# A two-layer mixture-of-experts encoder on one core: router logits with swapped operands, first masks and picks moved, warm-up matmuls at the head, new order of the tail

## Chip, cores and metric

The kernel runs on one core of one Trainium2 chip. The metric is the device time of one execution in microseconds (us), the median of three runs. All times below are us from the first instruction of one profiled execution unless they are marked otherwise.

## What is computed

512 tokens of width 1024 pass through two layers. Each layer has a mixing part (attention with dilated windows, gated MLP, pooling) and a routed expert part; all weights come from HBM. What matters here is the routing and the end of a layer:

```python
def _route(x_flat, router_w, router_bias):
    scores = jax.nn.sigmoid((x_flat @ router_w).astype(jnp.float32))
    biased = (scores + router_bias).reshape(T, N_EXPERT_GROUPS, EXPERTS_PER_GROUP)
    group_score = lax.top_k(biased, TOP_K)[0].sum(-1)
    gsel = jnp.argmax(group_score, axis=-1)
    in_group = biased[jnp.arange(T), gsel]
    _, local = lax.top_k(in_group, TOP_K)
    ...
    gates = sel / sel.sum(-1, keepdims=True)

def reference(x, ...):
    for l in range(DEPTH):                       # 2
        h = _mixing_sublayer(x, ...)
        x = _layernorm(DEEPNORM_ALPHA * x + h, ln1_g[l], ln1_b[l])
        h = _moe(x, router_w, router_bias, w_gate[l], w_up[l], w_down[l])   # 16 experts, top 2, SwiGLU, width 512
        x = _layernorm(DEEPNORM_ALPHA * x + h, ln2_g[l], ln2_b[l])
    return x
```

## The kernel before

Every large product is made of three passes in fp32r (`mm3`): a matrix is split into a rounded part and a remainder, and high times high, high times low and low times high are added in PSUM. ScalarE makes the rounded half of a weight piece (`emit_hi`, L184, tile `whi`), VectorE the remainder (`emit_lo`, L192, tile `wlo`). One half piece (128 x 1024) feeds six matmuls of 512 columns. There are four buffers of each (`NS = 4`), so the split of a half waits until TensorE has used the half four before it. All instructions are written out by hand in one order (a manual schedule): each engine works through its own in the order of the code, and waits where an operand is not there.

The head (L1182 on) loads the first inputs and weights and splits them; TensorE starts as they land.

Between mixing and experts stands the router, for four tiles of 128 tokens. `out2` finishes the output projection, `norm1(i)` normalises tile i and writes it to two places in DRAM. `logits(i)` turns the tile with eight transposes (L257), ScalarE copies them out of PSUM in two halves (L686), sixteen matmul passes in fp32 (eight products of two passes, L689) multiply with `router_w` as the weights loaded into the array (16 columns), and ScalarE takes the exponential of the 16 x 128 result. `scored` turns two such results back with a transpose each (L697) and VectorE adds 1 (L698). `route` ranks the experts on VectorE (some 13 small operations for two tiles), `place` counts positions with small matmuls, `pull(i)` adds tile i's rows of expert 0 into two PSUM banks (`b0`; 16 passes, L779). Then `early` makes the masks of experts 1 and 2 (`mark`, L770), calls `gates` (four operations on VectorE, L760 to L764, then four on GpSimd, L765 and L746 to L749, the last of which write the gate columns of `vg`), and for experts 1 and 2 picks the row numbers (`pick`, L841, four matmuls each, which read column 0 of `vg`) and starts the gathers of their rows from DRAM (L853, issued by GpSimd). `pull(3)` and `turn(0)` (expert 0's rows from PSUM into `gh`, `gl`) follow, then the expert loop.

In the loop, expert 0's `up_piece(0, 0)` and `(0, 1)` (24 matmuls) are followed by `front(1)` and `front(2)`: picks of three columns each, which read all of `vg`.

At the end of a layer the last two experts (14 and 15, `LAST`) are not scattered; `down_piece` writes their products to the two banks `bankY`, `finish_y` scales and splits them (L965 on ScalarE, L966 on VectorE), and `add_last` adds them per tile with matmuls and forms the LayerNorm's statistics, in a way given by `MODE`: "F" and "C" by `bn_stats` on VectorE, "P" by copying and squaring on ScalarE with sums (L1103, L1111) and two small GpSimd operations (L1112, L1113). `norm` scales and shifts. In the last layer `down_piece` of expert 15 runs the four halves for the first 512 columns, then for the second, and each normalised tile goes to `out`.

Of the kernel before, what the change touches and what calls it, by code (L numbers as in the profile page):

```python
# [59 lines left out]
def encoder(ctx, tc, a, out):  # L60
# [9 lines left out]
    LAST = (NE - 2, NE - 1)  # L70
    MODE = ("FPCC", "FFPP")
    cp = pool(ctx, "cp")
# [28 lines left out]
    def load_consts():  # L101
        nc.sync.dma_start(cb, a["consts"])
        nc.sync.dma_start(rw, a["router_w"])
        nc.sync.dma_start(rb, a["router_b"])
        G.memset(one16, 1.0)
        G.memset(mhalf, -0.5)
# [172 lines left out]
    def layer(l, xst, xh, xl, tail):  # L279
# [400 lines left out]

        eTs = {}

        def logits(i):
            xT = tp.tile([128, NK, 128], F32, name="rxT")
            for j in range(2):
                A.activation(xT[:, 4 * j:4 * j + 4, :], transpose4(bankT(), xs[i], j), AF.Copy)  # L686
            b = bankY()
            for k in range(NK):
                T.matmul(b[0:NE, 0:128], rw[:, k, :], xT[:, k, :], start=k == 0, stop=k == NK - 1)  # L689
            eTs[i] = rp.tile([NE, 128], F32, name="eT", bufs=4)  # L690
            A.activation(eTs[i], b[0:NE, 0:128], AF.Exp, scale=-1.0)

        def scored(i0, i1):
            b = bankY()
            bv = b[:, 0:NT * NE].rearrange("p (i e) -> p i e", e=NE)
            for i in range(i0, i1):
                T.transpose(bv[:, i, :], eTs.pop(i), ident[0:NE, 0:NE])  # L697
            V.tensor_scalar(sc[:, i0:i1], bv[:, i0:i1], 1.0, None, op0=OP.add)  # L698

# [20 lines left out]
        def route(i0, i1, E=V):  # L720
            n = i1 - i0
            g4 = lambda t: t[:, i0:i1].rearrange("p i (g e) -> p (i g) e", e=4)
            r = lambda t: t[:, i0:i1]
            E.reciprocal(r(sc), r(sc))
            E.tensor_tensor(r(bi), r(sc), rb[:, None, :].to_broadcast([128, n, NE]), op=OP.add)
            ranks(E, g4(rk), g4(bi), 4 * n)
            E.scalar_tensor_tensor(r(bi), r(rk), 1.5, r(bi), op0=OP.is_lt, op1=OP.mult)
            E.tensor_reduce(r(gs).rearrange("p i g -> p (i g)"), g4(bi), axis=AX.X, op=OP.add)
            ranks(E, r(gr), r(gs), n)
            E.tensor_scalar(r(gr), r(gr), 0.5, None, op0=OP.is_lt)  # L730
            grb = r(gr).rearrange("p i g -> p (i g)")[:, :, None].to_broadcast([128, 4 * n, 4])
            E.scalar_tensor_tensor(g4(m16), g4(rk), 1.5, grb, op0=OP.is_lt, op1=OP.mult)
# [52 lines left out]

        def norm1(i, between=None):
            stats = ln_stats(xs[i], tp)
            if between is not None:
                between()
            ln_apply(xs[i], gb1, stats, True)  # L790
# [145 lines left out]
        def down_piece(e, n):  # L936
            if n == 0:
                ES[e]["y"] = (bankY(), bankY())
            hh, hl = ES[e]["hT"]
            if e == NE - 1 and l + 1 == L:  # L940
                if n == 0:
                    w = [half(("e", l, e, 4 + k // 2), k % 2, NS - k) for k in range(4)]
                    for j in range(2):
                        ws = slice(j * 512, (j + 1) * 512)
                        for k in range(4):
                            mm3(ES[e]["y"][j][0:CAP], hh[:, k], hl[:, k], w[k][0][:, ws], w[k][1][:, ws], k == 0, k == 3)
                return
# [140 lines left out]

        def add_last(i):
            sums = None  # L1090
            if MODE[l][i] == "P":
                sums = sp.tile([128, 4], F32, name="sums", bufs=3)
            for j in range(2):
                js = slice(j * 512, (j + 1) * 512)
                b = bankT()
                if sums is not None:
                    T.matmul(b, ident, xs[i][:, js], start=True, stop=False)
                for e in LAST:
                    lhs = ES[e]["qT"][:, i * 128:(i + 1) * 128]
                    T.matmul(b, lhs, ES[e]["yl"][0][:, js], start=sums is None and e == LAST[0], stop=False)  # L1100
                    T.matmul(b, lhs, ES[e]["yl"][1][:, js], start=False, stop=e == LAST[1])
                if sums is not None:
                    A.activation(xs[i][:, js], b, AF.Copy, accum_out=sums[:, j:j + 1])  # L1103
                else:
                    V.tensor_tensor(xs[i][:, js], xs[i][:, js], b, op=OP.add)
            if sums is None:
# [7 lines left out]
            return None, t  # L1114

        stats = {}

        def prep(i):
# [3 lines left out]
            if MODE[l][i] == "C":  # L1122
                ln_center(xs[i], stats[i])

        def norm(i):
            if MODE[l][i] == "P":
                x, t = xs[i], stats[i][1]
                V.scalar_tensor_tensor(x, x, t[:, 2:3], gb2[0], op0=OP.add, op1=OP.mult)
                V.scalar_tensor_tensor(x, x, t[:, 1:2], gb2[1], op0=OP.mult, op1=OP.add)
            else:  # L1130
                ln_apply(xs[i], gb2, stats[i], MODE[l][i] == "F")

        prep(0)
        if l + 1 == L:
            for i in range(NT):
                prep(i + 1)
                norm(i)
                nc.sync.dma_start(out[i * 128:(i + 1) * 128, :], xs[i])
            ost.close()
            lst.close()  # L1140
            return None
        splits_to(stream["use"] + NS)
        norm(0)
# [162 lines left out]
```

## Time and profile before

| | |
|---|---|
| median of three runs | 1105.14 us (1104.51 to 1105.29) |
| profiled execution, its own time | 1104.96 us |
| span of its instructions | 1103.3 us |
| TensorE matmuls busy | 1055.1 us (96%) |
| VectorE, ScalarE, GpSimd busy | 883.8, 740.2, 413.7 us |
| mean granted TensorE clock | 0.994 |

The time is read from the chain of waits of TensorE: the other engines are free for a good part of the span, so an edit counts where it shortens or lengthens an idle stretch of TensorE, or what runs after its last matmul. A line of a timeline gives start, duration, engine, line, operation, written and read tiles with their shape, a count if equal instructions were merged, and in brackets how long the engine was idle before and whose end it waited for.

### The profile page before, as it was taken

The page shows a single profiled execution, that of the slowest core. Times are in us where ns is not written, and L with a number is a line of the kernel's source. Part 1 is how long each engine was busy: PE and PEld are TensorE (multiplying, and loading weights), DVE is VectorE, ACT ScalarE, POOL GpSimd, SP SyncE. Part 2 cuts the span into 40 slices and gives each one's busy share as a digit, 9 for nine tenths or more (in the row PEclk, how much of TensorE's full clock was granted, in tenths as well). Part 3 has the DMA queues.
Part 4 walks back from the last instruction along what each step waited for, and adds up shares of the span by engine and source line. Part 5 has one row for each costly group of instructions (what it writes and reads, how often), then busy time and mean ns, then how long its engine had stood idle before and what let it go on. Part 6 is the DMA issues. An engine that isn't in the chain of part 4 may idle for free.

```text
span 1103.3 us, 14619 instructions
## 1 busy us (share of the span) xinstructions
PE 1055.1 (96%) x5160; PEld 817.1 (74%) x5160; DVE 883.8 (80%) x1279; ACT 740.2 (67%) x1020; POOL 413.7 (37%) x325
## 2 busy tenths in 40 slices
PE   7999999999999999999899999899899999999995
PEld 5887776777777777777578877777777777777773
DVE  4433898879999999999756249878899999999996
ACT  4334877248888888888542358862578888888872
POOL 0294554232343525230125836433224343334102
PEclk9999999999999999999899999999999999999998
DMA  8162113979999999995313422249799999999831
GB/s 292 65 229 79 68 57 128 399 272 361 351 369 357 373 350 350 361 352 178 114 45 119 150 77 77 77 154 397 280 336 369 357 354 350 364 360 366 285 122 77
DMA packets 46943, 270.90 MB, mean 246 GB/s; under 512 B 8223, under 2 KB 8479, under 8 KB 19216
## 3 DMA queue, kind: packets, MB, share of 16 engines
q1 hardware_dynamic: 37152, 246.17, 59.4%
q0 software_dynamic: 8704, 19.75, 6.8%
q10 hardware_dynamic: 1008, 3.99, 1.0%
q8 instruction: 42, 0.69, 0.2%
q14 instruction: 37, 0.30, 0.1%
HBM read 257.62 MB, written 23.46 MB: 255 GB/s over the span
## 4 chain that ended last, share of the span: by engine, by line
PE 80%; ACT 8%; DVE 8%; issue 2%; DMA 1%; POOL 0%; SPq 0%; POOLq 0%; ACTq 0%; DVEq 0%
PE bA L218 17%; PE bA L216 17%; PE bA L217 17%; PE bY L216 6%; PE bY L217 6%; PE bY L218 6%; PE bT L263 3%; ACT pr L378 2%; ACT ph L212 1%; PE bA L779 1%; DVE pl L213 1%; DVE pr L371 1%; PE bY L689 1%; DVE kl L354 1%; ACT kh L353 1%
## 5 line engine op out<-in xcount | busy, mean ns | idle before, releaser
L192 DVE TENSOR_TENSOR wlo<-raw,whi 128x1024 fp32r<-128x1024 f32 x277 | 328.8, 1224 | 93.4 <-ACT whi L184 90.5
L184 ACT ACTIVATE whi<-raw 128x1024 fp32r<-128x1024 f32 x283 | 295.7, 1060 | 102.6 <-PE bA L218 67.9
L853 POOL DMA_INDIRECT xs<-x1d,si x26 | 129.1, 4964 | 279.2 <-DVE sg L848 243.7
L216 PE MATMUL bA<-whi,gh 128*112 128x512 f32 x512 | 204.4, 399 | 3.8 <-ACT gh L212 2.7
L218 PE MATMUL bA<-whi,gl 128*112 128x512 f32 x512 | 201.7, 394 | 0.2
L217 PE MATMUL bA<-wlo,gh 128*112 128x512 f32 x512 | 200.7, 392 | 0.0
L216 PE MATMUL bA<-whi,xh 128*128 128x512 f32 x256 | 104.4, 408 | 8.3 <-ACT whi L212 7.8
L216 PEld LDWEIGHTS bA<-whi,gh 128*112 128x112 f32 x512 | 89.1, 174 | 31.4 <-ACT gh L212 3.1
L218 PEld LDWEIGHTS bA<-whi,gl 128*112 128x112 f32 x512 | 89.2, 174 | 31.0 <-DVE gl L213 1.9
L217 PEld LDWEIGHTS bA<-wlo,gh 128*112 128x112 f32 x512 | 89.1, 174 | 27.1
L218 PE MATMUL bA<-whi,xl 128*128 128x512 f32 x256 | 102.5, 400 | 0.0
L217 PE MATMUL bA<-wlo,xh 128*128 128x512 f32 x256 | 102.3, 400 | 0.0
L387 POOL TENSOR_SCALAR pr<-pr,nm 128x512 f32<-128x512 f32 x42 | 67.6, 1617 | 90.8 <-DVE nm L385 75.5
L216 PE MATMUL bY<-whi,hh 128*112 128x512 f32 x240 | 96.5, 402 | 0.0
L218 PE MATMUL bY<-whi,hl 128*112 128x512 f32 x240 | 94.5, 394 | 0.0
L217 PE MATMUL bY<-wlo,hh 128*112 128x512 f32 x240 | 94.3, 393 | 0.0
L858 POOL DMA_INDIRECT accd<-y,si x28 | 56.1, 2004 | 68.8 <-ACT y L971 61.5
L216 PEld LDWEIGHTS bA<-whi,xh 128*128 128x128 f32 x256 | 48.9, 191 | 21.2 <-ACT whi L212 8.6
L192 DVE TENSOR_TENSOR wlo<-qkt,whi 128x1024 fp32r<-128x1024 f32 x48 | 57.1, 1220 | 3.4 <-ACT whi L184 3.4
L192 DVE TENSOR_TENSOR wlo<-pr,whi 128x1024 fp32r<-128x1024 f32 x48 | 57.3, 1220 | 1.4 <-ACT whi L184 1.3
L217 PEld LDWEIGHTS bA<-wlo,xh 128*128 128x128 f32 x256 | 48.8, 191 | 12.8 <-DVE wlo L213 0.9
L218 PEld LDWEIGHTS bA<-whi,xl 128*128 128x128 f32 x256 | 48.6, 190 | 12.4 <-DVE xl L213 0.9
(249 smaller groups left out, 2085.6 us busy)
## 6 DMA issues: line engine op xcount, KB each, us to landing
raw<-w_exp SPq DMA_DIRECT2D x116, 1024.0 KB, 11.9
raw<-w_mix SPq DMA_DIRECT2D x24, 1024.0 KB, 4.8
qkt<-w_exp SPq DMA_DIRECT2D x24, 1024.0 KB, 11.6
pr<-w_exp SPq DMA_DIRECT2D x24, 1024.0 KB, 11.0
er<-w_exp SPq DMA_DIRECT2D x12, 1024.0 KB, 8.0
px<-w_exp SPq DMA_DIRECT2D x12, 1024.0 KB, 10.9
x1d<-xs POOLq DMA_DIRECT2D x8, 512.0 KB, 8.3
accd<-xs SPq DMA_DIRECT2D x8, 512.0 KB, 10.0
```

Source lines behind the costliest of these rows:

```text
L184: A.activation(hi, raw, AF.Copy)
L192: (eng or V).tensor_tensor(lo, raw, hi, op=OP.subtract)
L212: A.activation(hi, src, AF.Copy)
L213: V.tensor_tensor(lo, src, hi, op=OP.subtract)
L216: T.matmul(ps, xh, wh, start=start, stop=False)
L217: T.matmul(ps, xh, wl, start=False, stop=False)
L218: T.matmul(ps, xl, wh, start=False, stop=stop)
L263: T.transpose(t[:, c * CAP:(c + 1) * CAP], src[0:CAP, (4 * j + c) * 128:(4 * j + c + 1) * 128], ident[0:CAP, 0:CAP])
L378: A.activation(pr[:, i, :], pr[:, i, :], AF.Exp, bias=nm[:, 0, i:i + 1], scale=-1.0, accum_out=nm[:, 1, i:i + 1])
L387: E.tensor_scalar(pr[:, i, :], pr[:, i, :], nm[:, 2, i:i + 1], None, op0=OP.mult)
L853: G.indirect_dma_start(out=dst[0:CAP], out_offset=None, in_=xd[l][:, :], in_offset=bass.IndirectOffsetOnAxis(ap=idx, axis=0), bounds_check ...
L858: G.indirect_dma_start(out=accd[l][:, :], out_offset=bass.IndirectOffsetOnAxis(ap=idx, axis=0), in_=src[0:CAP], in_offset=None, bounds_che ...
```

## The change

Head: 48 matmuls of a constant 128 x 128 tile with itself are put ahead of the first real one; VectorE fills that tile instead of GpSimd.

Router: the logits are formed with the turned tokens as the loaded weights and `router_w` as the 16 moving columns, so that the result already lies with tokens in partitions; `scored` is gone and `route` adds 1 itself. The transposes of a tile stand one tile ahead of its logits; `norm1(3)` and all logits come before the first `route`; `route(2, 4)` stands before the pulls of tiles 0 and 1.

Behind the router: `emit_lo`, the masks of experts 1 and 2 and `pull(3)`, `emit_lo` and `turn(0)` come first, then the picks and gathers of experts 1 and 2 (`early`), then the splits of two more weight halves, and only then `gates`.

End of a layer: `down_piece` of expert 15 uses banks of the four-bank pool `bankA`. In the last layer it runs the first 512 columns in its first piece and the second 512 in its second, the four tiles' statistics are all formed with sums (new mode "A": VectorE adds and sums in one operation; "P" as before), and the additions of tiles 0 and 1 are ordered by halves.

```diff
-    MODE = ("FPCC", "FFPP")
+    MODE = ("FPCC", "AAPP")
...
+        def turn_x(i):
+            xTs[i] = tp.tile([128, NK, 128], F32, name="rxT")
+            for j in range(2):
+                A.activation(xTs[i][:, 4 * j:4 * j + 4, :], transpose4(bankT(), xs[i], j), AF.Copy)
         def logits(i):
-            xT = tp.tile([128, NK, 128], F32, name="rxT")
-            for j in range(2):
-                A.activation(xT[:, 4 * j:4 * j + 4, :], transpose4(bankT(), xs[i], j), AF.Copy)
-            b = bankY()
+            xT, b = xTs.pop(i), bankY()
             for k in range(NK):
-                T.matmul(b[0:NE, 0:128], rw[:, k, :], xT[:, k, :], start=k == 0, stop=k == NK - 1)
-            eTs[i] = rp.tile([NE, 128], F32, name="eT", bufs=4)
-            A.activation(eTs[i], b[0:NE, 0:128], AF.Exp, scale=-1.0)
-        def scored(i0, i1):
...
+                T.matmul(b[:, 0:NE], xT[:, k, :], rw[:, k, :], start=k == 0, stop=k == NK - 1)
+            A.activation(sc[:, i], b[:, 0:NE], AF.Exp, scale=-1.0)
...
+            E.tensor_scalar(r(sc), r(sc), 1.0, None, op0=OP.add)
             E.reciprocal(r(sc), r(sc))
...
-        for i in range(2):
+        norm1(3)
+        turn_x(0)
+        turn_x(1)
+        logits(0)
+        turn_x(2)
+        for i in (1, 2):
             logits(i)
-        norm1(3, emit_lo)
+        turn_x(3)
+        logits(3)
+        route(0, 2)
...
-        logits(2)
-        scored(0, 2)
-        route(0, 2)
-        logits(3)
         place(0, 2)
-        scored(2, 4)
+        route(2, 4)
         pull(0)
         pull(1)
-        route(2, 4)
         place(2, 4)
         pull(2)
...
         def early():
-            for e in (1, 2):
-                ES[e] = {"q": mark(pm[:, :, e])}
-            gates()
-            emit_lo()
             for e in (1, 2):
                 idx, _ = pick((ES[e]["q"],), lambda i: vg[:, i, e, 0:1], "f", 2, 1)
                 gather(xgs[e % 2], idx)
...
             if n == 0:
-                ES[e]["y"] = (bankY(), bankY())
+                bank = bankA if e == LAST[1] else bankY
+                ES[e]["y"] = (bank(), bank())
...
-        early()
+        emit_lo()
+        for e in (1, 2):
+            ES[e] = {"q": mark(pm[:, :, e])}
         pull(3)
+        emit_lo()
         rst.close()
         PO["ep"] = pool(lst, "ep", 2, side="right")
         turn(0)
+        early()
         rxs["bufs"] = 1
         splits_to(stream["use"] + NS)
+        gates()
         ahead()
...
+            elif sums is not None:
+                V.scalar_tensor_tensor(xs[i][:, js], xs[i][:, js], 1.0, b, op0=OP.mult, op1=OP.add,
+                                       accum_out=sums[:, j:j + 1])
...
         if l + 1 == L:
-            for i in range(NT):
-                prep(i + 1)
-                norm(i)
+            sums = [new_sums(i) for i in range(2)]
+            for j in range(2):
+                for i in range(2):
+                    add_half(i, j, sums[i], (bankT, bankY)[j])
+            for i in range(2):
+                stats[i] = spread(i, sums[i])
+            def sent(i):
+                scale(i)
                 nc.sync.dma_start(out[i * 128:(i + 1) * 128, :], xs[i])
+            for i in range(2):
+                n = i + 2
+                sums.append(new_sums(n))
+                for j in range(2):
+                    add_half(n, j, sums[n], (bankT, bankY)[i])
+                if i == 0:
+                    center(0)
+                    center(1)
+                else:
+                    sent(0)
+                    sent(1)
+                stats[n] = spread(n, sums[n])
+            for i in range(2, NT):
+                center(i)
+                sent(i)
...
+        heat = bankT()
         warm = ip.tile([128, 1], F32, name="warm")
+        V.memset(one16, 1.0)
...
+        for _ in range(48):
+            T.matmul(heat[:, 0:128], one16, one16, start=True, stop=True)
```

## Rows read from the trace of the kernel before

**Rows 1.** Page: busy time, share of the span, instructions of TensorE

```profile
PE 1055.1 (96%) x5160; PEld 817.1 (74%) x5160; DVE 883.8 (80%) x1279; ACT 740.2 (67%) x1020; POOL 413.7 (37%) x325
```

**Rows 2.** Waits of TensorE in the whole span: total us, times, longest

```profile
PE bA L216 <- ACT whi L212: 7.8, 2, 5.5
...
PE bY L216 <- DVE er L966: 3.7, 2, 1.9
...
PE bY L257 <- DVE xs L245: 2.6, 1, 2.6
```

**Rows 3.** Windows: length, busy us (count) by engine, granted clock, DMA share, GB/s

```profile
9.70:14.10 4.40, 4.31 (x10) 3.10 (x11) 3.24 (x4) 3.21 (x4) 0.00 (x0) 1.00 1.02 409
...
526.70:529.50 2.80, 0.94 (x4) 0.49 (x4) 2.80 (x5) 2.52 (x4) 0.00 (x0) 1.00 0.03 12
...
529.50:533.00 3.50, 3.50 (x11) 2.52 (x10) 1.88 (x2) 1.06 (x1) 0.00 (x0) 0.52 0.00 0
...
1073.40:1079.00 5.60, 5.60 (x24) 4.24 (x25) 2.44 (x3) 1.06 (x2) 0.00 (x0) 1.00 0.02 3
```

**Rows 4.** TensorE's timeline, router of layer 0: start, us, line, tiles, idle before

```profile
218.50 1.92 PE L689 MATMUL bY<-rxT,rw 128*16 128x128 f32 x16 [0.31 <-ACT rxT L686]
...
220.35 1.10 PE L257 MATMUL bT<-cb,xs 128*128 128x128 f32 x8
...
226.86 0.29 PE L697 MATMUL bY<-cb,eT 16*128 16x16 f32 x2
...
228.49 1.92 PE L689 MATMUL bY<-rxT,rw 128*16 128x128 f32 x16 [0.31 <-ACT rxT L686]
...
231.53 3.83 PE L779 MATMUL bA<-q,xs 128*128 128x112 f32 x32 [0.47 <-DVE q L770]
...
238.10 0.53 PE L841 MATMUL bA<-vg,qslot 128*112 128x1 f16 x8
...
246.12 0.53 PE L841 MATMUL bA<-vg,qslot 128*112 128x3 f16 x8
```

**Rows 5.** VectorE's timeline behind the router of layer 0

```profile
237.16 0.22 DVE L760 TENSOR_TENSOR gf<-m,sc 128x64 f32<-128x64 f16 x1
...
237.97 1.20 DVE L192 TENSOR_TENSOR wlo<-er,whi 128x1024 fp32r<-128x1024 f32 x1
...
244.35 3.49 DVE L192 TENSOR_TENSOR wlo<-qkt,whi 128x1024 fp32r<-128x1024 f32 x3
```

**Rows 6.** GpSimd's timeline behind the router of layer 0

```profile
238.14 1.17 POOL L765 TENSOR_TENSOR gf<-gf,gsum 128x64 f32<-128x64 f32 x1 [12.43 <-DVE gsum L764]
...
240.16 0.46 POOL L749 TENSOR_SCALAR vg<-spg 128x64 f16<-128x64 f32 x1
...
242.66 1.51 POOL L853 DMA_INDIRECT xs<-x1d,fi  x1 [0.30 <-issue]
...
270.76 5.43 POOL L853 DMA_INDIRECT xs<-x1d,si  x1 [4.00 <-DVE sg L848]
```

**Rows 7.** VectorE's timeline under the last of these gathers

```profile
270.67 4.62 DVE L192 TENSOR_TENSOR wlo<-raw,whi 128x1024 fp32r<-128x1024 f32 x4
```

**Rows 8.** VectorE's timeline, end of layer 0

```profile
529.32 1.21 DVE L192 TENSOR_TENSOR wlo<-raw,whi 128x1024 fp32r<-128x1024 f32 x1
...
537.06 1.40 DVE L966 SCALAR_TENSOR_TENSOR y<-bY,sg,gl 112x512 fp32r<-112x512 f32 x2
```

**Rows 9.** VectorE's timeline, end of layer 1

```profile
1073.87 1.22 DVE L192 TENSOR_TENSOR wlo<-raw,whi 128x1024 fp32r<-128x1024 f32 x1
...
1094.92 1.28 DVE L1128 SCALAR_TENSOR_TENSOR xs<-xs,lnt,qkt 128x1024 f32<-128x1024 f32 x1
...
1096.64 1.28 DVE L1129 SCALAR_TENSOR_TENSOR xs<-xs,lnt,qkt 128x1024 f32<-128x1024 f32 x1 [0.44 <-POOL lnt L1113]
```

**Rows 10.** ScalarE's timeline, end of layer 1

```profile
1088.88 1.15 ACT L1111 ACTIVATE y<-xs,lnt 128x1024 f32<-128x1024 f32 x1 [0.28 <-DVE lnt L1109]
```

**Rows 11.** GpSimd's timeline, end of layer 1

```profile
1093.79 1.27 POOL L1112 TENSOR_SCALAR lnt<-sums 128x1 f32<-128x1 f32 x1 [1.68 <-ACT y L1111]
```

More of the change, by code (lines that the diff above doesn't have):

```diff
@@ L104, in load_consts @@
         nc.sync.dma_start(rb, a["router_b"])
-        G.memset(one16, 1.0)
         G.memset(mhalf, -0.5)
@@ L679, in layer @@
         load_ln(l, "ln1", gb1)
[L681 removed]
+        xTs = {}
+        def turn_x(i):
+            xTs[i] = tp.tile([128, NK, 128], F32, name="rxT")
+            for j in range(2):
+                A.activation(xTs[i][:, 4 * j:4 * j + 4, :], transpose4(bankT(), xs[i], j), AF.Copy)
         def logits(i):
[L684 to L687 removed]
+            xT, b = xTs.pop(i), bankY()
             for k in range(NK):
[L689 to L698 removed]
+                T.matmul(b[:, 0:NE], xT[:, k, :], rw[:, k, :], start=k == 0, stop=k == NK - 1)
+            A.activation(sc[:, i], b[:, 0:NE], AF.Exp, scale=-1.0)
         pm = rtp.tile([128, NT, NE], F32, name="pm")
@@ L784, in out2, with norm1 @@
             out_unit(w[2 * nh:2 * nh + 2], HS["catA"], i, nh, 1.0, b)()
-        def norm1(i, between=None):
+        def norm1(i):
             stats = ln_stats(xs[i], tp)
-            if between is not None:
-                between()
             ln_apply(xs[i], gb1, stats, True)
@@ L941, in down_piece @@
                 if n == 0:
[L942 to L946, printed above, removed]
+                    ES[e]["w"] = [half(("e", l, e, 4 + k // 2), k % 2, NS - k) for k in range(4)]
+                w = ES[e]["w"]
+                ws = slice(n * 512, (n + 1) * 512)
+                for k in range(4):
+                    mm3(ES[e]["y"][n][0:CAP], hh[:, k], hl[:, k], w[k][0][:, ws], w[k][1][:, ws], k == 0, k == 3)
                 return
@@ L1086, in layer, with add_half, new_sums, spread @@
                         load_ln(l, "ln2", gb2)
[L1089 to L1105, printed above, removed]
+        def add_half(i, j, sums, bank=bankT):
+            js = slice(j * 512, (j + 1) * 512)
+            b = bank()
+            keep = MODE[l][i] == "P"
+            if keep:
+                T.matmul(b, ident, xs[i][:, js], start=True, stop=False)
+            for e in LAST:
+                lhs = ES[e]["qT"][:, i * 128:(i + 1) * 128]
+                T.matmul(b, lhs, ES[e]["yl"][0][:, js], start=not keep and e == LAST[0], stop=False)
+                T.matmul(b, lhs, ES[e]["yl"][1][:, js], start=False, stop=e == LAST[1])
+            if keep:
+                A.activation(xs[i][:, js], b, AF.Copy, accum_out=sums[:, j:j + 1])
+            elif sums is not None:
+                V.scalar_tensor_tensor(xs[i][:, js], xs[i][:, js], 1.0, b, op0=OP.mult, op1=OP.add,
+                                       accum_out=sums[:, j:j + 1])
+            else:
+                V.tensor_tensor(xs[i][:, js], xs[i][:, js], b, op=OP.add)
+        def new_sums(i):
+            return sp.tile([128, 4], F32, name="sums", bufs=3) if MODE[l][i] in "PA" else None
+        def spread(i, sums):
             if sums is None:
@@ L1114, in add_last @@
             return None, t
+        def add_last(i):
+            sums = new_sums(i)
+            for j in range(2):
+                add_half(i, j, sums)
+            return spread(i, sums)
         stats = {}
@@ L1123, in prep, with center, scale @@
                 ln_center(xs[i], stats[i])
+        def center(i):
+            V.scalar_tensor_tensor(xs[i], xs[i], stats[i][1][:, 2:3], gb2[0], op0=OP.add, op1=OP.mult)
+        def scale(i):
+            V.scalar_tensor_tensor(xs[i], xs[i], stats[i][1][:, 1:2], gb2[1], op0=OP.mult, op1=OP.add)
         def norm(i):
[L1126 to L1129, printed above, removed]
+            if MODE[l][i] in "PA":
+                center(i)
+                scale(i)
             else:
                 ln_apply(xs[i], gb2, stats[i], MODE[l][i] == "F")
-        prep(0)
         if l + 1 == L:
-            for i in range(NT):
-                prep(i + 1)
-                norm(i)
-                nc.sync.dma_start(out[i * 128:(i + 1) * 128, :], xs[i])
+            sums = [new_sums(i) for i in range(2)]
[5 more added lines that the diff above has]
+            def sent(i):
+                scale(i)
+                nc.sync.dma_start(out[i * 128:(i + 1) * 128, :], xs[i])
+            for i in range(2):
+                n = i + 2
+                sums.append(new_sums(n))
+                for j in range(2):
+                    add_half(n, j, sums[n], (bankT, bankY)[i])
+                if i == 0:
+                    center(0)
+                    center(1)
+                else:
+                    sent(0)
+                    sent(1)
+                stats[n] = spread(n, sums[n])
+            for i in range(2, NT):
+                center(i)
+                sent(i)
             ost.close()
@@ L1141, in layer @@
             return None
+        prep(0)
         splits_to(stream["use"] + NS)
```

## Prediction, made before the changed kernel ran

> **What bounds the kernel now.** I read the page first: TensorE is busy for 1055.1 of 1103.3 us [rows 1], so an edit pays where it takes an idle stretch of TensorE away, or shortens what follows its last matmul. Then TensorE's waits over the whole span, which name the stretches: 7.8 us in two pieces at the head for the first split weights (the longer 5.5, so the other 2.3); twice 1.9 us, once in each layer, for VectorE to read the bank that expert 15 wants; one of 2.6 us at the end of layer 0 for a normalised tile [rows 2]. Then the same places by windows, for the clock [rows 3]: ten matmuls of 512 columns in 4.31 us at the head (0.43 each, the pace of 1.2 GHz, though the clock column says 1.00), against 24 in 5.60 near the end (0.23 each, the pace of 2.4 GHz). At the end of layer 0 the idling of 1.9 us is followed by 3.5 us with a granted clock of 0.52, that of 2.6 us by another such stretch, so 3.5 x 0.48 = 1.7 us is lost behind each. At the end of layer 1 the same 1.9 us was followed by a clock of 1.00. So idling of about 2 us may cost the clock or not, and 2.6 us did. Last the timelines of the router stretch [rows 4 to 7], which comes twice, 544.5 us apart with the same shape, and of the two layer ends [rows 8 to 11].
>
> The sum is made against the profiled execution's 1104.96 us (span 1103.3 and 1.7 around it); the median is 0.2 above it, which I add at the end.
>
> **Head.** 48 matmuls of 128 columns at a quarter of 0.43 us are 5.1 us, from about 1.2 to 6.3. The first real matmul comes at 5.5 (the end of the longest wait) and may be pushed to 6.3; behind it lies the wait of 2.3 us for the next split, which hides that. If the full clock held from then on, eight of the ten matmuls would gain 0.2 each, 1.7 us. But between warm-up and 9.7 at least 2.3 us of idling stay, between the 1.9 and the 2.6 that were followed by half clock. I take two matmuls' gain, **-0.4** (0 to -1.7).
>
> **Router logits.** Swapping operands frees little on TensorE: sixteen passes stood at 1.85 us (218.50 to 220.35 [rows 4]) with 16 columns of weights and 128 moving; now 128 columns of weights are loaded per pass and 16 move. The nearest row is L697, two fp32 loads of 128 columns with 16 moving: 226.86 to 227.09, 0.115 each, so 16 x 0.115 = 1.84. What goes is waiting: per tile 1.41 us lie between one tile's logits and the next's (220.35 + 1.41 = 221.76), of which eight transposes are 0.86 and 0.55 the copy by ScalarE. One tile ahead, that copy is covered by other logits. New order, from 218.50: second half of tile 1's transposes until 219.45; logits 1.84, transposes 0.86, twice logits 3.68, transposes 0.86, a wait of 0.55 (the last tile has no cover), logits 1.84: 229.1. Before: 228.49 + 1.85 = 230.3. `route(0, 2)` now ends on VectorE before that, so `place` and the pulls follow in about 1.0 instead of 1.2: 230.05 against 231.53. The second ranking and the pulls keep their 4.7 us (pull 2 began 1.85 before the picks at 238.10). The early picks, 0.4 us, leave the way to `pull(3)` but return in front of the first expert matmul. I count the first 24 expert matmuls done at 244.8 where the next picks stood at 246.1 [rows 4], after 0.1 to 0.3 for banks still being read: **-1.3 per layer, -2.6** (-1.6 to -4.4; the large end if loads of weights cost half of L697's).
>
> **Gates behind the gathers.** This is what the sum hangs on. `front(1)`, behind those 24 matmuls, reads all of `vg`. Before, GpSimd wrote `vg` by 240.62 (240.16 + 0.46), 5.5 us ahead of it [rows 6]. Now GpSimd's queue has both gathers first, and the gates' VectorE operations stand behind two weight splits. Working: the last pull ends at 238.45, `turn(0)` and the two row numbers on VectorE 1.45 later, 239.9 (an estimate: a copy and a subtraction for each bank). Gathers of 1.15 to 1.5 us with 0.3 between them [rows 6] last until about 243. VectorE: two splits of 1.17 (3.49 / 3 [rows 5]) from 240.15, then the gates' four operations of about 0.2, the first 0.22: 243.3. Then three splits for halves 4 to 6 stand back to back until 246.8, because all of their inputs are there; after them VectorE itself waits for `front(1)`. How do the four GpSimd operations run beside them? L765 with 64 columns took 1.17 us under a split that ended at 239.17, and itself ended 0.14 behind it [rows 5, 6]: it waits for VectorE's instruction to end. L1112 in the tail started at 1093.79 and ended at 1095.06, just behind the 1094.92 where one VectorE instruction followed another without a gap [rows 9, 11]: one GpSimd operation gets through per boundary. So they end at 244.6, 245.8, 247.0 and, with VectorE idle, 247.5; the picks can start at 247.7 instead of 244.8. TensorE idles **2.9 us**, more than the 2.6 that was followed by half clock, so I add 1.7. Per layer +4.6, **+9.2** in all. Nothing behind takes it back: in the expert loop TensorE is the bound. Bounds: +0.5 per layer if GpSimd is not held at all (243 + 1.5 + 0.3 = 245.3 at the earliest), +6.6 if a gather is held as at 270.76 below. The SP queue's loads come after `gates` in the code but wait for none of it.
>
> A rule of the Trainium skill bears on the four operations: the page "SBUF — State Buffer", section "SBUF: two separate sides", calls the port pair of VectorE and GpSimd an exclusive lock, held for a whole instruction, with the other fully blocked. By that rule a gather too is held for one split only, which is the sum above; by the row of 270.76 it is held longer, which is the second rival. No row shows which of the two holds for the first gathers under three splits.
>
> **End of layer 0.** Expert 15's first matmul no longer waits 1.9 us for the bank; the last of its four weight halves is split by 530.5 (529.32 + 1.21 [rows 8]), before it needs that at 531. With the idling goes, I think, the stretch at 0.52. Twenty-four matmuls from 526.8 end at 532.4. Late next is VectorE: behind the split for half 3 stand three for the next layer, then the remainders of expert 15 (L966, 537.06 before [rows 8]); these can now start at 533.9. **-3.1** (-1.3 if the clock falls anyway, -3.3). The idling of 2.6 us after it stays, with its half clock.
>
> **End of layer 1.** Here the order by columns needs all four halves within 12 matmuls, and the fourth's remainder ends at 1075.09 (1073.87 + 1.22 [rows 9]). So of the 1.9 us only 0.55 comes back. The additions then run without a stall, but four squares on ScalarE (1.15 [rows 10] and a readout) stand where two stood, and each tile's two small GpSimd operations run beneath VectorE instructions, 1.3 and about 1.5 us [rows 11]. Laid out from these: the sums of tiles 0 and 1 are there at 1083.4, squares and the copies of tiles 2 and 3 fill ScalarE until 1092.7, VectorE, at 1.28 a pass [rows 9], has centred tile 3 by 1095.15, the power operation held beneath it ends 0.4 later, and the last scaling starts at 1095.6 instead of 1096.64: **-1.1** (-0.3 to -2.1, the latter if GpSimd is never late).
>
> Sum: -0.4 - 2.6 + 9.2 - 3.1 - 1.1 = +2.0: 1107.0, by the median 1107.1 (0.18 added, rounded).
>
> **Rivals.** First, faster: GpSimd is not held. For it: the second early gather took only 1.51 us although splits ran beside it [rows 6]. Against it: L765. Then the idling is 0.5 per layer, without half clock: -7.2 + 1.0 on 1104.96 and the median's 0.2, **1098.9**; halfway cases lie up to 1102. Second, slower: a gather is starved. At 270.76 one took 5.43 us while four splits ran back to back for 4.62 [rows 6, 7], and ended 0.9 after the last. If the first or second gather starts under a split that others follow without a gap, it ends near 247.7, the gates at 249.4, and TensorE idles 4.9 + 1.7 per layer: +13.2 - 7.2, **1111.1**. It decides on whether the first gather starts before the split at 240.15; I have it 0.2 earlier. Third, the change doesn't do what it says: the warm-up cannot bridge to 9.7, the freed bank in layer 0 leaves the clock falling (-1.3), the tail's squares cost what the order gains (-0.3): 1104.96 - 2.6 + 9.2 - 1.6, **1110.1**.
>
> **How the numbers follow.** Forecast 0.46 (own range 1104 to 1109.5), GpSimd free 0.30, starved 0.14, not doing what it says 0.10. A measurement of this kernel can tell about 0.2%, 2.2 us, from no change: faster is below 1102.9, slower above 1107.4. Faster: 0.29 of the first rival, 0.01 of the forecast: 0.30. Same: 0.28 of the forecast, 0.01 of the first rival: 0.29. Slower: 0.17 of the forecast and both others: 0.41. The range runs from the first rival's time, 1099, to 1111.5, just above the second's; about 0.13 lies below and 0.06 above.
>
> **What would show it.** After the change, right or wrong: TensorE's waits should have a line for the picks (L841) behind GpSimd, once per layer, near 3 us, and the windows a clock near 0.5 behind it; GpSimd's timeline shows gathers ahead of the gates and each gate operation ending with a VectorE instruction. If the picks wait less than 1 us, the forecast is wrong by the first rival. The wait for `er` must be gone in layer 0 and about 1.3 us, for a remainder, in layer 1. At the head, the matmuls from 11 us on show 0.43 or 0.23. The logits of a tile should still take about 1.8 us.

## The result: 0.74% slower than before, and the profile after

The changed kernel takes 1113.22 us (median of seven runs, 1109.14 to 1114.86) where the kernel before took 1104.56 beside it (seven runs, 1103.62 to 1105.29): a ratio of 1.0074, with a 95% interval of 1.0065 to 1.0084. The forecast was 1107.1, its range ended at 1111.5. The profiled execution took 1112.28 us with a span of 1110.6, against 1104.96 and 1103.3. I read it in the order in which the profile before was read; "answers [rows 1]" marks the view after the change that stands against those rows.

The page, busy time of the engines (answers [rows 1]):

```profile
PE 1065.0 (96%) x5200; PEld 833.1 (75%) x5200; DVE 882.4 (79%) x1280; ACT 742.1 (67%) x1024; POOL 418.3 (38%) x324
```

TensorE has 40 instructions more (48 dummy matmuls, less 8 small transposes), and is busy for 9.9 us more. The dummies are 4.4 of these, in time that was idle before; the other 5.5 are matmuls that take longer. So a good part of the loss is not idling. Its waits over the span (answers [rows 2]; engine, bank and line, whose end it waited for, total us, times, longest):

```profile
PE bA L836 <- POOL vg L744: 5.4, 2, 2.7
...
PE bY L256 <- DVE xs L244: 2.6, 1, 2.6
PE bA L215 <- ACT whi L211: 1.7, 1, 1.7
```

The first line is the forecast's wait of the picks (L841 before, L836 now) for the gates on GpSimd, once per layer. The wait for `er` (3.7 us in [rows 2]) is gone, the head waits 1.7 where it waited 7.8 in two pieces (the dummy matmuls fill the first). The windows (answer [rows 3]; length, busy us of TensorE, its weight loads, VectorE, ScalarE, GpSimd, then the granted clock):

```profile
8.50:14.20 5.70, 5.47 (x22) 4.23 (x23) 4.34 (x4) 4.24 (x4) 0.00 (x0) 1.00 1.02 388
214.00:222.90 8.90, 8.59 (x77) 8.19 (x76) 7.81 (x14) 3.75 (x9) 3.12 (x4) 1.00 1.01 415
222.90:233.10 10.20, 9.49 (x48) 9.10 (x46) 4.80 (x23) 1.45 (x4) 0.00 (x0) 0.50 0.75 278
...
245.70:250.20 4.50, 1.83 (x14) 1.50 (x14) 3.28 (x9) 1.05 (x1) 3.66 (x5) 1.00 0.96 310
250.20:253.60 3.40, 3.40 (x9) 2.41 (x8) 2.17 (x3) 1.66 (x2) 0.00 (x0) 0.50 1.02 348
...
769.00:782.70 13.70, 12.99 (x64) 12.60 (x64) 6.56 (x29) 1.75 (x5) 0.63 (x1) 0.50 0.70 265
```

The pair at 245.7 and 250.2 is the idling and the half clock behind it that the forecast had. The stretches of 10.2 us from 222.9 (layer 0) and 13.7 us from 769.0 (layer 1) at 0.50, the level of 1.2 GHz, it did not have: they begin in the router while TensorE is busy, in layer 0 for 8.59 of the 8.90 us ahead. TensorE's timeline there (answers [rows 4]), from the first transposes of tile 0 to those of expert 1's rows:

```profile
214.16 1.04 PE L256 MATMUL bT<-cb,xs 128*128 128x128 f32 x8
...
219.10 3.64 PE L691 MATMUL bY<-rw,rxT 128*128 128x16 f32 x32
222.60 1.69 PE L256 MATMUL bT<-cb,xs 128*128 128x128 f32 x8
224.18 3.59 PE L691 MATMUL bY<-rw,rxT 128*128 128x16 f32 x16
...
228.54 6.00 PE L774 MATMUL bA<-q,xs 128*128 128x112 f32 x32 [0.71 <-DVE q L765]
...
248.37 0.53 PE L836 MATMUL bA<-vg,qslot 128*112 128x3 f16 x8 [2.71 <-POOL vg L744]
...
255.94 0.93 PE L262 MATMUL bT<-cb,xs 112*128 112x112 f32 x8
```

In layer 0 the logits of tiles 1 and 2 take 1.8 us each, as before. Those of tile 3 take 3.59, the transposes ahead of them 1.69 where [rows 4] has 1.10, and the pulls of tiles 0 and 1 6.00 where [rows 4] has 3.83. A table by stage, from the starts of the same operations in both timelines; the two that bound the router of layer 0 stand above for the kernel after, and for the kernel before they are:

```profile
217.16 1.04 PE L257 MATMUL bT<-cb,xs 128*128 128x128 f32 x8
...
252.12 0.93 PE L263 MATMUL bT<-cb,xs 112*128 112x112 f32 x8
```

| from, to | before, us | after, us | difference |
|---|---|---|---|
| start to first transposes of tile 0, layer 0 | 217.16 | 214.16 | -3.0 |
| these to the transposes of expert 1's rows (router) | 34.96 | 41.78 | +6.8 |
| these to expert 0's down products | 15.84 | 15.79 | 0.0 |
| these to the first addition at the end of layer 0 | 268.03 | 264.34 | -3.7 |
| this to tile 0 of layer 1 | 225.73 | 226.22 | +0.5 |
| router of layer 1 | 34.97 | 43.43 | +8.5 |
| rest to the end of the span | 306.59 | 304.89 | -1.7 |
| sum | | | +7.3 |

The head, both layer ends and the tail became faster, 7.9 us together in these two executions. The router stretch became 15.3 us slower.

### The profile page after: what moved, and what is told of

Its sections match the earlier page's. It is cut to its first block, busy times and chain, and to the rows that moved or that the text cites. A ratio compares the mean times of both kernels' runs of the same rounds, so it can differ in the third digit from the quotient of the medians.

```text
span 1110.6 us, 14702 instructions
## 1 busy us (share of the span) xinstructions
PE 1065.0 (96%) x5200; PEld 833.1 (75%) x5200; DVE 882.4 (79%) x1280; ACT 742.1 (67%) x1024; POOL 418.3 (38%) x324
## 4 chain that ended last, share of the span: by engine, by line
PE 80%; ACT 8%; DVE 7%; POOL 2%; issue 2%; DMA 1%; POOLq 0%; SPq 0%; ACTq 0%; DVEq 0%
PE bA L217 17%; PE bA L215 17%; PE bA L216 17%; PE bY L215 6%; PE bY L217 6%; PE bY L216 5%; PE bT L262 3%; PE bA L774 2%; PE bY L691 2%; ACT pr L377 2%; ACT ph L211 1%; DVE pl L212 1%; DVE pr L370 1%; ACT whi L183 1%; DVE kl L353 1%
## 5 line engine op out<-in xcount | busy, mean ns | idle before, releaser
L215 PE MATMUL bA<-whi,gh 128*112 128x512 f32 x528 | 212.2, 402 | 4.2 <-ACT gh L211 2.7
L216 PE MATMUL bA<-wlo,gh 128*112 128x512 f32 x528 | 208.3, 395 | 0.8 <-DVE wlo L191 0.8
L215 PEld LDWEIGHTS bA<-whi,gh 128*112 128x112 f32 x528 | 92.6, 175 | 34.2 <-ACT gh L211 3.1
L216 PEld LDWEIGHTS bA<-wlo,gh 128*112 128x112 f32 x528 | 92.8, 176 | 29.0 <-DVE wlo L191 1.1
L183 ACT ACTIVATE whi<-pr 128x1024 fp32r<-128x1024 f32 x48 | 50.9, 1061 | 18.1 <-PE bA L217 14.7
## 6 DMA issues: line engine op xcount, KB each, us to landing
raw<-w_exp SPq DMA_DIRECT2D x116, 1024.0 KB, 11.9
er<-w_exp SPq DMA_DIRECT2D x12, 1024.0 KB, 10.5
```

The lines of the kernel that those rows point to most:

```text
L183: A.activation(hi, raw, AF.Copy)
L215: T.matmul(ps, xh, wh, start=start, stop=False)
L216: T.matmul(ps, xh, wl, start=False, stop=False)
```

## Experiments

Theory A: the swapped operands, with 16 moving columns in a pass, let TensorE's clock fall in the router. Rival B: the new order lets it fall (less waiting between the logits, the later pulls). Rival A2: loading 128 columns of weights for each pass does. Apart from that: the gates behind the gathers cost what the forecast said, and they do because VectorE's splits hold GpSimd up. Each median is set against that of the kernel before, run beside it (1103.78 to 1104.56), since these differ by up to 0.8 us; where an expectation says -9.3, its two medians are from two sittings, and that difference is 8.5 when each is taken against its own neighbour:

| kernel | median, us | to before, us | ratio (95%) |
|---|---|---|---|
| changed | 1113.22 | +8.7 | 1.0074 (1.0065 to 1.0084) |
| wide moving columns | 1103.89 | +0.1 | 0.9997 (0.9985 to 1.0010) |
| swap alone | 1114.39 | +10.5 | 1.0093 (1.0077 to 1.0109) |
| logits as before | 1109.39 | +5.6 | 1.0046 (1.0029 to 1.0063) |
| gates first | 1103.95 | +0.2 | 1.0011 (0.9993 to 1.0029) |
| logits as before, gates first | 1100.47 | -3.3 | 0.9968 (0.9957 to 0.9980) |
| wide, late gates on VectorE | 1096.72 | -7.4 | 0.9941 (0.9926 to 0.9956) |
| router as before | 1098.25 | -5.6 | 0.9942 (0.9925 to 0.9958) |
| warm-up alone | 1102.86 | -1.0 | 0.9990 (0.9981 to 1.0000) |
| wide, gates first | 1093.85 | -10.0 | 0.9915 (0.9901 to 0.9929) |
| the same, filled | 1094.02 | -10.2 | 0.9919 (0.9905 to 0.9932) |

**Operands swapped, but 128 moving columns**

```diff
-    rw = cp.tile([128, NK, NE], F32, name="rw")
+    rw2 = cp.tile([128, 2 * NK, NE], F32, name="rw")   # router_w twice
...
-                T.matmul(b[:, 0:NE], xT[:, k, :], rw[:, k, :], ...)
+                T.matmul(b[:, 0:NK * NE], xT[:, k, :], rw2[:, k:k + NK, :].rearrange(...), ...)
```

> The changed kernel with the operands swapped as changed, but 128 moving columns in each pass: router_w lies twice in SBUF, and product k takes the eight blocks from block k on, so that its first 16 result columns are the logits and the other 112 are not read. Tells the number of moving columns from the side the tokens stand on. Theory A, few moving columns let the clock fall: the stretches at 0.5 in the router are gone and a tile's logits take 1.85 to 2.0: about 1101. Theory A2, loading 128 columns of weights for each pass lets it fall, however many columns move: they stay, 1112. Theory B (order): they stay, 1112.

Measured: 1103.89 us (ten runs, 1100.95 to 1108.00), level with the kernel before, so 8.5 us less than the changed kernel. TensorE's timeline of this kernel in the router of layer 0, then windows of both routers and of its head:

```profile
222.43 3.74 PE L692 MATMUL bY<-rw,rxT 128*128 128x128 f32 x32
...
227.35 2.05 PE L692 MATMUL bY<-rw,rxT 128*128 128x128 f32 x16 [0.31 <-ACT rxT L686]
```

```profile
217.00:245.00 28.00, 25.88 (x205) 23.19 (x204) 22.70 (x54) 11.14 (x19) 7.53 (x9) 1.00 0.79 305
763.00:791.00 28.00, 25.80 (x204) 23.03 (x203) 22.80 (x54) 11.19 (x20) 7.63 (x8) 1.00 0.79 304
...
8.80:15.60 6.80, 6.45 (x15) 4.76 (x16) 5.32 (x5) 4.53 (x5) 0.00 (x0) 0.50 1.03 399
```

The clock is 1.00 through both routers, in the same order and with the same loads of 128 columns: A2 and B fall. It is so in every trace with swapped operands: with 128 moving columns (this kernel and three below) the clock stays at 1.00 through the logits and pulls of both layers, with 16 (the changed kernel and two below) it falls there in both. A tile's logits cost nearly the same with 128 moving columns as with 16 (3.74 and 3.64 us for two). The median stays 3 us above the 1101 of theory A, which took half of the two stretches, 11.9 us, for the price of the fall; by the lengths of the routers, given with the account of the prediction, it is 8.7. The profiled execution, at 1107.88 one of the two slowest of the ten, also has 6.8 us at half clock in the head, which the changed kernel's does not have (the row above against its 8.50 to 14.20).

**The swapped operands alone**

```diff
-                T.matmul(b[0:NE, 0:128], rw[:, k, :], xT[:, k, :], start=k == 0, stop=k == NK - 1)
+                T.matmul(b[:, 0:NE], xT[:, k, :], rw[:, k, :], start=k == 0, stop=k == NK - 1)
...                                                    # scored gone, route adds 1; all else as before
```

> The kernel before with the logits' operands swapped alone (16 moving columns, no scored, VectorE adds 1 in route); order, gates, head, ends as before. Theory A, few moving columns let the clock fall: stretches at 0.5 begin in or right behind the logits of both layers, 5 to 7 us per layer: 1104 + 10 to 14 = 1114 to 1118. Rival: it falls only where the logits stand close together as in the new order; here transposes lie between any two of them, and the clock holds: 1104 less the two transposes of a pair, about 1103.

Measured: 1114.39 us, 10.5 above the kernel before, the lower end of theory A. Timeline and windows of the router of layer 0:

```profile
220.12 2.98 PE L688 MATMUL bY<-rw,rxT 128*128 128x16 f32 x16 [0.25 <-ACT rxT L685]
222.94 1.95 PE L257 MATMUL bT<-cb,xs 128*128 128x128 f32 x8
224.78 3.59 PE L688 MATMUL bY<-rw,rxT 128*128 128x16 f32 x16
```

```profile
215.60:220.80 5.20, 4.64 (x39) 4.12 (x38) 5.17 (x8) 2.36 (x5) 2.02 (x3) 1.00 1.00 403
220.80:237.80 17.00, 16.29 (x79) 15.61 (x79) 8.30 (x30) 2.94 (x7) 1.78 (x2) 0.50 0.70 260
```

So this one edit makes the kernel before 10 us slower, without any of the new order, and it does so in the second tile's logits already. The third tile's logits wait no longer for ScalarE's copy, because the transposes ahead of them now take 1.95: waits shrink as work slows.

**The logits as before, in the new order**

```diff
-                T.matmul(b[:, 0:NE], xT[:, k, :], rw[:, k, :], start=k == 0, stop=k == NK - 1)
+                T.matmul(b[0:NE, 0:128], rw[:, k, :], xT[:, k, :], start=k == 0, stop=k == NK - 1)
...
         turn_x(3)
+        scored(0, 2)
         logits(3)
...
         place(0, 2)
+        scored(2, 4)
         route(2, 4)
```

> The changed kernel with one part undone: the logits have router_w as the loaded weights and the turned tokens as 128 moving columns again, with the two transposes back (`scored`); the new order (transposes a tile ahead, masks, picks and gates late) stays. Theory A, the swapped operands (16 moving columns in a pass) let TensorE's clock fall in the router: the stretches at 0.5 that begin at 222.90 (10.24 us) and 769.03 (13.65 us) are gone, half of their length comes back, 23.9 / 2 = 11.9, less 2 x 0.3 for the transposes: the profiled 1112.3 becomes about 1101. Theory B, the new order lets it fall (transposes and logits without a pause, or the later pulls): the stretches stay, 1112 to 1113. Both: the picks still wait 2.7 us for GpSimd per layer, with 3.4 us at 0.5 behind.

Measured: 1109.39 us, 3.1 less than the changed kernel (5.6 against 8.7 above before), not 11. The windows show what of theory A holds here:

```profile
231.70:235.10 3.40, 3.40 (x18) 3.40 (x17) 2.31 (x11) 0.00 (x0) 0.00 (x0) 0.50 0.48 195
766.80:798.30 31.50, 26.02 (x206) 21.75 (x205) 23.24 (x59) 11.15 (x18) 10.63 (x11) 1.00 0.76 282
```

In layer 1 the clock stays at 1.00 through the logits and until behind the picks. In layer 0 it falls behind the logits, for a third of the time. And a new wait stands there in both layers, here in layer 0:

```profile
230.23 0.18 PE L744 MATMUL bY<-m,tri 128*128 128x16 f16 x1 [1.41 <-DVE m L735]
```

Tile 1's result is now turned back only behind tile 3's transposes, the first ranking starts on VectorE with it, and `place` waits for its end. So the edit does not undo one thing cleanly: it removes the long half clock and puts 1.41 us of waiting, twice, and a shorter half clock in its place. The routers are 41.41 and 39.78 us long, where the changed kernel's are 41.78 and 43.43. The expectation had overlooked that in the new order nothing covers the ranking.

**Gates ahead of the picks and gathers**

```diff
             ES[e] = {"q": mark(pm[:, :, e])}
+        gates()
         pull(3)
...
         splits_to(stream["use"] + NS)
-        gates()
```

> The changed kernel with `gates` ahead of the early picks and gathers again, right behind the two masks; all else as changed. Theory: the gates behind the gathers cost 2.7 us of waiting and 1.7 us of half clock per layer, 8.8 in all: 1112.3 becomes 1103.5, and no wait of the picks for GpSimd over 0.3 us. Rival: the wait only hides another (the first gather now comes later, and expert 1's rows are turned later): 1108 or more, with a wait of the transposes of expert 1's rows in place of it. The router's stretches at 0.5 stay in both.

Measured: 1103.95 us (ten runs, 1101.34 to 1110.79, two of them above 1109), 8.5 less than the changed kernel where 8.8 was expected. No wait of the picks on GpSimd is left; the half clock in the router is (10.2 us at 0.50 from 222.5 in layer 0). GpSimd's timeline shows the same operations as in the changed kernel. Only the first still lies beneath a split (238.48 to 239.67) and ends 0.16 behind it; the next lie beside operations of VectorE that read a PSUM bank (L212):

```profile
238.66 1.17 POOL L760 TENSOR_TENSOR gf<-gf,gsum 128x64 f32<-128x64 f32 x1 [16.41 <-DVE gsum L759]
239.89 0.29 POOL L741 CAST vg<-gf 128x64 f16<-128x64 f32 x1
240.27 0.32 POOL L743 TENSOR_TENSOR spg<-gf,vg 128x64 f32<-128x64 f32 x1
```

**Both: logits as before, gates first.** The two edits above together.

> Logits as before and `gates` ahead of the gathers, together; head, order of transposes and logits, bank and tail as changed. Theory A with the price of the gates: both gains add, 1112.3 - 11.3 - 8.8 = 1092. Theory B: only the gates' 8.8 come, 1103.5. If the two losses overlap (the clock falls anyway for one of them), 1096 to 1100.

Measured: 1100.47 us. The two gains add (3.1 and 8.5 make 11.6, measured 8.7 + 3.3 = 12.0), but the first is the small one measured, not the 11.3 that the expectation had summed.

**The late gates, on VectorE.** With wide moving columns, the gates in their late place:

```diff
-            G.tensor_tensor(gf, gf, gsum[:, :, None].to_broadcast([128, NT, NE]), op=OP.mult)
-            split_gate(vg[:, :, :, 1], vg[:, :, :, 2], gf, G)
+            V.tensor_tensor(gf, gf, gsum[:, :, None].to_broadcast([128, NT, NE]), op=OP.mult)
+            split_gate(vg[:, :, :, 1], vg[:, :, :, 2], gf)
```

> The kernel with wide moving columns (median 1103.9) with the gates still late and behind the gathers, but with their last four operations on VectorE instead of GpSimd. Theory, GpSimd's operations each wait for the end of a split beneath which they run: on VectorE they take about 0.2 each, between the reciprocal (ended 243.5 in that kernel's trace) and the three splits, and `vg` is there at 244.3, ahead of the picks' 245.07: no wait over 0.3, no stretch at 0.5 behind it, 1103.9 - 8.8 = 1095. Rival, the late place is the cause whichever engine does them (their operands, or the two splits ahead of them, come too late): the picks still wait 1 us or more, 1099 to 1104.

Measured: 1096.72 us, against 1103.89 with GpSimd. VectorE's timeline, then TensorE's at the picks and a wait that is new:

```profile
240.92 0.22 DVE L746 TENSOR_SCALAR vg<-spg 128x64 f16<-128x64 f32 x1
241.03 3.49 DVE L192 TENSOR_TENSOR wlo<-qkt,whi 128x1024 fp32r<-128x1024 f32 x3
```

```profile
241.54 0.53 PE L838 MATMUL bA<-vg,qslot 128*112 128x3 f16 x8
```

```profile
PE bA L218 <- DVE gl L213: 1.4, 2, 0.7
```

The place behind two splits is early enough: `vg` is there at 241.14, and the picks start without a wait. What cost the 2.7 us is that GpSimd did it beneath the splits. The time is 1.7 us above the 1095 expected, and 2.6 above that of the fastest kernel below when each is taken against its neighbour. TensorE's new wait is 0.7 per layer, for expert 1's remainder on VectorE; in layer 1 of this trace it is followed by 3.5 us at a clock of 0.55. From the first transposes to expert 0's down products the two layers are 50.09 and 51.66 us long, in that fastest kernel 49.57 and 49.55, so 0.5 and 2.1 more.

**The router as before, all else changed.** Warm-up, bank of expert 15 and tail as changed; logits, order, `early` and the place of the gates as before.

> The changed kernel with its whole router as before (logits with router_w as weights, scored, early with gates ahead of the gathers, the old order); warm-up, bank of expert 15 and tail as changed. What is worth what, from the two traces: the end of layer 0 -3.2 (-3.7 until the additions, +0.5 behind), the end of layer 1 -1.7, the head -3.0 if the full clock holds from 4.4 us on, 0 if it falls in the idling behind the warm-up: 1104.5 - 4.9 - (0 to 3) = 1096.6 to 1099.6. So by theory the head and the two ends give 5 to 8 us and the router alone makes the change slower. Rival, the two ends only look faster because the layer runs late (loads are further ahead when TensorE comes later): then 1102 or more.

Measured: 1098.25 us, inside what the stages gave. So the head and the ends are worth 5.6 us, and the router's part turned that into a loss.

**The warm-up alone**

```diff
-        G.memset(one16, 1.0)
...
+        V.memset(one16, 1.0)
...
+        for _ in range(48):
+            T.matmul(heat[:, 0:128], one16, one16, start=True, stop=True)
         first(0)
```

> The kernel before with the 48 warm-up matmuls alone. As the forecast had it (the idling of some 2 us behind the first three matmuls drops the clock again): -0.4, 1103.6. As the changed kernel's trace shows it (full clock from 4.4 us on, ten matmuls and more at 0.23): -3.0, 1101. As the runs with the logits back and with wide moving columns show it (0.5 again from about 9 us for 3.4 or 6.8 us): -0.5 to +0.3. Theory: it differs from run to run, a median of 1102 to 1103 and a spread of some 3 us.

Measured: 1102.86 us (ten runs, 1100.11 to 1104.22): -1.0 in the median, with an interval that reaches no change, and with a spread of 4 us where the kernel before, beside it, has 1.6. In its trace the clock falls again behind an idling of 2.25 us:

```profile
10.90:14.30 3.40, 3.40 (x10) 2.64 (x9) 3.31 (x3) 2.96 (x3) 0.00 (x0) 0.51 1.03 405
```

**Wide moving columns and gates first**

> The changed kernel with 128 moving columns in the logits and with gates ahead of the early picks: both losses taken away. Medians so far: 1113.2 changed, -9.3 by wide columns, -9.3 by the gates. If they are separate: 1094.6, and no stretch at 0.5 between the transposes of tile 0 and expert 2 in either layer. Rival, they overlap (the half clock behind the picks and that in the router are partly the same time): 1097 to 1100. If the new order itself costs time in the router, it is slower than the kernel with the whole router as before, run beside it.

Measured: 1093.85 us, so the two losses are separate: the rival had 1097 to 1100. The sum was right within 0.8 us; taken against their neighbours the two gains of 8.5 would leave 1095.5, and the kernel is 1.7 below that. In this trace the clock falls nowhere ahead of the last microseconds. This is the fastest version, 0.85% under the kernel before. The router of layer 0 in windows:

```profile
214.20:226.00 11.80, 11.18 (x98) 10.62 (x97) 9.02 (x21) 4.90 (x11) 3.12 (x4) 1.00 1.02 386
226.00:236.00 10.00, 8.39 (x84) 8.12 (x81) 8.31 (x26) 1.24 (x4) 1.26 (x2) 1.00 0.48 193
```

Its router stretches are 34.29 and 33.72 us long, where the kernel with the old router, run beside it, has 34.95 and 35.01. So the new order and the swapped operands, without the two losses, are worth 0.7 and 1.3 us. The 0.7 holds a new wait of 0.43 us for expert 1's gather, behind which the next stage is 0.5 shorter; with that stage taken in, it is 1.2 us in each layer.

**The same, with dummy matmuls in two idle stretches.** 18 behind the first three real matmuls, 27 ahead of tile 0's turning at the end of layer 0.

> Wide moving columns and gates first (median 1093.85), with dummy 128 x 128 matmuls in two idle stretches of TensorE: 18 behind the first three real matmuls (idle 6.83 to 8.51), 27 ahead of the first turned tile at the end of layer 0 (idle 535.57 to 538.16). If idling of that length is what lets the clock fall in some runs, no run has a stretch at 0.5 there: 0 to 1.7 us less at each, median about 1092.5, smaller spread. Rival: the dummies end after the operand they wait beside and push real work: 0.3 to 1 us more, 1094.5.

Measured: 1094.02 us, no difference. Its clock is 1.00 over both places, but so it was in the trace without dummies, which left nothing to win in that execution. The 27 dummies took 1.68 us of the 2.6. Whether filling pays where the clock does fall stays open.

## Why the prediction was wrong, and where it was right

**Router logits: the step that failed.** The forecast counted what the swap does to the passes' time and found nothing, rightly: 1.8 us per tile, at full clock. It took the clock to depend on idling alone ("With the idling goes, I think, the stretch at 0.52", at the end of layer 0), and asked of the router only how long TensorE waits there. The runs show a second way: the clock fell to 0.50 with TensorE busy for 8.59 of 8.90 us, in passes of 16 moving columns, and did not with 128 in the same passes. In the rows before there was no stretch like it; L697, from which the price was taken, was two instructions long. Price: the router stretches with gates first are 37.54 and 39.21 us long with 16 columns and 34.29 and 33.72 with 128, so 3.3 and 5.5, together 8.7 (by the medians 8.5 with the gates late, 10.2 with them first). No rival had it either. Without the fall the term itself held: -0.7 and -1.3, and -1.2 each with the next stage, where -1.3 per layer was forecast (-1.6 to -4.4 for both).

**Gates behind the gathers: right in place, mechanism and size.** Forecast: TensorE idles 2.9 us and loses 1.7 behind. Measured: 2.71 and 2.73 (layer 1), then 3.4 and 3.5 us at half clock; 8.5 us in the medians (10.1 between the two kernels with wide columns) where the sum had 9.2. GpSimd's timeline of the changed kernel (answers [rows 6]), then VectorE's over the same time (answers [rows 5]):

```profile
240.84 1.11 POOL L848 DMA_INDIRECT xs<-x1d,fi  x1 [18.78 <-DVE fi L838]
242.24 1.85 POOL L848 DMA_INDIRECT xs<-x1d,fi  x1 [0.30 <-DVE wlo L191]
244.12 1.20 POOL L760 TENSOR_TENSOR gf<-gf,gsum 128x64 f32<-128x64 f32 x1
245.38 1.17 POOL L741 CAST vg<-gf 128x64 f16<-128x64 f32 x1
246.63 1.12 POOL L743 TENSOR_TENSOR spg<-gf,vg 128x64 f32<-128x64 f32 x1
247.84 0.47 POOL L744 TENSOR_SCALAR vg<-spg 128x64 f16<-128x64 f32 x1
```

```profile
243.95 3.62 DVE L191 TENSOR_TENSOR wlo<-qkt,whi 128x1024 fp32r<-128x1024 f32 x3
```

The three splits end at about 245.2, 246.4 and 247.6 (3.62 / 3 each); the three operations beneath them end at 245.32, 246.55 and 247.75, each some 0.2 behind. The conversion that takes 1.17 here takes 0.29 with the gates first. The rival in which GpSimd is free needed such short ones; the rival in which a gather is starved did not come true, the gathers took 1.11 and 1.85. The Trainium skill's rule (page "SBUF — State Buffer", section "SBUF: two separate sides": one side holds the shared port pair for a whole instruction and the other waits) agrees with these ends.

**Head: inside the bounds in the median; the profiled gain is in part luck.** Forecast -0.4 (to -1.7). By the run with the warm-up alone it is -1.0 in the median, with an interval that reaches no change. The changed kernel's trace has -3.0: there the clock stayed full over an idling of 1.66 us, and TensorE started on the second split weights at 8.49 where the kernel before did at 9.79. How early they come differs between executions: in the trace of the swap alone, whose head is that of the kernel before, it started on them at 8.39, and the router begins at 215.65 and not at 217.16. So the profiled -3.0 is not to be put into a sum against medians.

**End of layer 0: right in mechanism, in size with some luck.** Forecast -3.1; -3.7 until the first addition, of which 0.5 is lost behind it, so -3.2. The wait for the bank is gone. But 1.5 of the 3.7 hangs on the one execution of the kernel before: with the warm-up alone, where this layer end is as before, the same wait of 1.86 us was not followed by half clock, and the stage is 266.51 us long instead of 268.03. The idling of 2.6 us later, and the half clock behind it, stayed.

**End of layer 1: right, a little low.** Forecast -1.1 (to -2.1), measured -1.7. The wait for the fourth half's remainder is 0.8, not the 1.3 of the forecast; from expert 0's down products to the first addition the stage went from 266.49 to 265.35, so 1.1 came back where the forecast had 0.55. That is the 0.6.

Put together with the sizes as measured in the profiles: -3.0 for the head, -1.9 for the order of the logits, +8.7 for the clock in the router, +8.5 for the gates (the changed kernel's two router stretches less those with gates first), -3.2 and -1.7 for the ends are +7.4, and the span grew by 7.3. The three terms of the router must add up, since each is the difference between neighbours in one row of kernels (before, wide with gates first, gates first, changed). With the head's -1.0 from the medians in place of -3.0 the sum is +9.4, where the medians differ by 8.7. Without the fall of the clock in the router the changed kernel takes 1103.89, which lies in the forecast's range and 3.2 below its time; of these, 1.4 are the kernel before, which took 1103.78 in that sitting and not 1105.14.

What stays open: the fastest kernel is 4.4 us below the one with the old router, 2.0 of it by the router stretches. In the two profiles the rest is half clock behind idling, which the first has nowhere ahead of its last microseconds and the second in the head and at the end of layer 0. Why its five runs (mean granted clock 0.995 to 0.996, against 0.993 to 0.995) avoid that more often was not tried. Nor was a number of moving columns between 16 and 128, or 16 with fewer columns of weights.

## What to carry to other kernels

A matmul's operands are not interchangeable even where both forms take the same time: look at the granted clock of the stretch, and keep the long side moving (or widen the short one, as here, where 128 moving columns cost nearly what 16 did). An operation on GpSimd that someone waits for belongs where VectorE has gaps; beneath a row of splits each one costs a split. Where a change mixes gains and losses, time its parts alone: here 5.6 us of gain lay beneath two losses of 8 to 10 us each.

## What the hardware showed that was not expected

- TensorE's granted clock fell to 0.50 for 10 to 17 us in each layer while TensorE was 93 to 96% busy, with 16 moving columns in fp32 passes; with 128 it stayed at 1.00.
- The cost of a pass at full clock hardly depended on the moving columns: 32 passes took 3.64 us with 16 and 3.74 with 128 (0.114 and 0.117 each), with 128 columns of weights loaded for each.
- The idling behind the first real matmuls, with the warm-up ahead, was of different length in each execution: 1.0 to 1.8 us kept the full clock in five traces and lost it in one (1.47), 2.3 us lost it in three of three. The idling of 2.7 us ahead of the picks was followed by half clock in both layers of all three kernels that had it. Whether this is what gave the warm-up alone its spread of 4 us was not measured.
